# Sliding-window attention: one transposed weight tile for two key blocks, and another order for the last heads

## The chip, the cores and the metric

The kernel runs on one core of one Trainium2 chip. The metric is the device time of one execution in microseconds (us); of the kernel before, three executions are shown. The engines are named as the profile names them: PE (TensorE, matmul and transpose), PEld (its weight loads), DVE (VectorE), ACT (ScalarE), POOL (GpSimd) and SP (SyncE, which here only issues DMAs).

## The reference

The program is a decoder trunk of two layers on 1024 tokens of width 1024, all in float32. Layer 0 (RWKV-7 time mixing beside a gated MLP) isn't touched. Layer 1 is sliding-window attention with 16 query heads, 2 key/value heads, ALiBi and a learned sink per head, followed by a SiLU gate, an output projection and the final norm:

```python
q, k, v, z = jnp.split(p, [ODD_MIX, ODD_MIX + KV_W, ODD_MIX + 2 * KV_W], axis=-1)
...
dist = qi + WINDOW - kj          # qi: 0..127, kj: 0..255 (previous block, own block)
valid = (dist >= 0)[None] & (dist < WINDOW)[None] & (key_pos >= 0)
scores = scores - slopes * dist
scores = jnp.where(valid, scores, -jnp.inf)
m = jnp.maximum(jnp.max(scores, axis=-1, keepdims=True), sink)
e = jnp.exp(scores - m)
probs = e / (jnp.sum(e, axis=-1, keepdims=True) + jnp.exp(sink - m))
out = jnp.einsum('bnhgqk,bnkhd->bnqhgd', probs, v_band)
y = out * jax.nn.silu(z)
return y @ w_out
```

A block of 128 queries sees two blocks of 128 keys: the one before it and its own. Query i may use key j of the previous block only where j > i, and key j of its own block only where j <= i. So for each pair (i, j) at most one of the two weights differs from zero.

## The kernel before, in words

The change lies in layer 1, which is the last 350 us of the span. Everything is float32; a matmul operand is split into a high and a low part (`hi`/`lo`, `PH`/`PL`, `KH`/`KL`) of type float32r, and three (or two) matmuls of parts make one product.

**Tiles.** Tokens are handled in two halves of 512 (`half`), query heads in 8 pairs (`n`, two heads `e` each). `head_projs(n)` (L1361) loads the weight columns of the pair with `wload` (two DMAs of 256 KB on SP into `wraw`, of which there are three buffers; per DMA one ACT copy to `whi`, L257, and one subtraction on POOL to `wlo`, L258) and projects queries (`qproj`) and gates (`zgate`), each as 24 matmuls of 512 columns per half (`pproj`).

**One attention block** is (head pair, half, block of 128 queries), 64 in all. `attend` (L1285 on) does, for each:

1. scores: 4 matmuls `pS`;
2. bias, minimum and row maximum: 2 operations on DVE (L1305), from PSUM to `Sx`;
3. exponential with row sum: 2 on ACT (L1309);
4. reciprocal of the sums on DVE (L1311), then the scaling by it on POOL, 2 operations over all 256 keys (L1313);
5. transposes on PE, one per head and key block, 4 of 128x128 (L1319; 2 in the first block of the sequence, which has no previous block), into PSUM tile `pT`;
6. split of `pT`, 512 columns: `PH` on ACT (L1324), `PL = pT - PH` on DVE (L1325);
7. weighted sum with the values: 4 matmuls `po` of 256 columns (`PH` and `PL`, times previous and own block of `VV`; L130 is the line of the helper for all matmuls).

After two blocks, the four quadrants of `po` are put together by ACT and DVE (`cm`, L1334 to L1337) and multiplied into `y` on POOL (L1339).

**What sets the order.** A scheduler puts the instructions of each engine in one fixed order when the program is built; `attend` has high priority, so its matmuls stand between those of the projections of the next pair. At run time each engine takes its instructions in that order and waits at each for semaphores. With `N1 = 4`, half 1 of pairs 4 to 7 is attended only after all projections. The output weights (`wo`, two halves of 512 columns in `hi`/`lo` tiles that replace those of layer input `h`) are loaded after that, 8 pieces of 256 KB each (L1396 to L1398; ACT makes `hi`, POOL or DVE by turns makes `lo`). The output projection (`op`, 24 matmuls per 128 tokens and half of the columns) fills PE between the last attention blocks, and stands alone at the end.

## Time and profile before

| | |
|---|---|
| three executions | 1092.3, 1091.01, 1091.95 us; median 1091.95 us |
| the profiled execution | 1086.66 us, span 1084.8 us |
| busy in the span | PE 96%, PEld 77%, DVE 64%, ACT 48%, POOL 34% |
| transposes of attention weights on PE (L1319) | 240, mean 272 ns |
| weight scaling on POOL (L1313) | 128 |
| first score matmul, last weighted sum | at 734.8 and 1030.6 us of the span |

A row of the views that group instructions gives line, engine, operation, output tile <- input tiles and shape, the count, then the busy time in us and the mean duration in ns, then the idle time of the engine before them and what ended it. Matmuls overlap in the array: a row's mean is the duration of one, and the distance of two starts in the timeline is what one costs.

### The profile page before, as it was taken

To read this page: it belongs to the slowest core of one execution; us is meant where nothing else is said; L and a number is where in the kernel's file an instruction comes from. 1 tells how busy PE (TensorE), PEld (TensorE's weight loads), DVE (VectorE), ACT (ScalarE), POOL (GpSimd) and SP (SyncE) were. 2 spreads that over 40 slices of the span, in tenths; PEclk is the share of its full clock that TensorE was granted. 3 is DMA by queue.
4 is the path that set the end of the run, shared out by engine and by line. 5 is a ranking of instruction groups with operands and counts; after the bars stand their busy time and mean duration, and the time that the engine had idled before them with its cause. 6 is when DMAs were issued, how large, how long until landed. Compare 5 with 4: busy or idle time off the path is not lost.

```text
span 1084.8 us, 20721 instructions
## 1 busy us (share of the span) xinstructions
PE 1039.3 (96%) x7887; PEld 834.1 (77%) x7888; DVE 694.0 (64%) x1668; ACT 521.5 (48%) x1247; POOL 370.2 (34%) x483
## 2 busy tenths in 40 slices
PE   6989989998999899999999999999999999999997
PEld 3667767777777677777888787778888888878886
DVE  4355868595868585858433688755565544488753
ACT  4464464544454546454423223336665644486521
POOL 2233323232323233233344100225455544467201
PEclk9989999999999999999999999999999999999998
DMA  9601121212121122212213655411011011251221
GB/s 363 238 18 40 60 79 59 70 50 69 64 86 57 60 68 70 69 53 84 91 61 124 184 183 177 146 45 40 23 37 40 20 40 40 98 165 59 75 81 59
DMA packets 55131, 93.42 MB, mean 86 GB/s; under 512 B 5748, under 2 KB 15988, under 8 KB 55032
## 3 DMA queue, kind: packets, MB, share of 16 engines
q1 hardware_dynamic: 45176, 77.36, 21.5%
q10 hardware_dynamic: 9856, 14.75, 4.2%
q8 instruction: 62, 1.02, 0.4%
q14 instruction: 37, 0.30, 0.1%
HBM read 79.49 MB, written 12.59 MB: 85 GB/s over the span
## 4 chain that ended last, share of the span: by engine, by line
PE 52%; DVE 4%; ACT 2%; issue 1%; DMA 1%; POOL 1%; ACTq 0%; POOLq 0%; DVEq 0%; SPq 0%
PE pproj L130 24%; PE op L130 16%; PE po L130 2%; PE pS L130 2%; PE pT L1319 2%; PE htp L134 1%; PE pM L130 1%; PE py L130 0%; DVE pr L728 0%; DMA wraw<-y0d 0%; PE mix L130 0%; DVE Sx L1305 0%; PE mq L130 0%; PE gvn L130 0%; PE uw L130 0%
## 5 line engine op out<-in xcount | busy, mean ns | idle before, releaser
L130 PE MATMUL pproj<-hi,whi 128*128 128x512 f32 x696 | 281.1, 404 | 0.7 <-ACT vt L1273 0.7
L130 PE MATMUL pproj<-hi,wlo 128*128 128x512 f32 x696 | 280.7, 403 | 0.0
L130 PE MATMUL pproj<-lo,whi 128*128 128x512 f32 x696 | 280.6, 403 | 0.0
L258 POOL TENSOR_TENSOR wlo<-wraw,whi 128x512 fp32r<-128x512 f32 x86 | 114.8, 1353 | 155.2 <-ACT whi L257 154.3
L130 PEld LDWEIGHTS pproj<-hi,whi 128*128 128x128 f32 x696 | 131.4, 189 | 27.8 <-issue 3.6
L130 PEld LDWEIGHTS pproj<-hi,wlo 128*128 128x128 f32 x696 | 131.3, 189 | 26.0 <-issue 2.4
L130 PEld LDWEIGHTS pproj<-lo,whi 128*128 128x128 f32 x696 | 131.5, 189 | 25.0 <-issue 1.7
L130 PE MATMUL op<-wo,whi 128*128 128x512 f32 x256 | 81.1, 397 | 0.1
L257 ACT ACTIVATE whi<-wraw 128x512 fp32r<-128x512 f32 x102 | 59.0, 622 | 37.2 <-issue 13.5
L1309 ACT ACTIVATE Sx<-Sx,nm 128x257 f32<-128x257 f32 (+1 forms) x128 | 62.3, 489 | 27.3 <-DVE nm L1305 25.3
L1305 DVE CUSTOM_DVE_ANT_0 Sx<-pS,bias,nsink 128x256 f32<-128x256 f32 (+1 forms) x128 | 53.5, 463 | 30.0 <-PE pS L130 28.6
L1313 POOL TENSOR_SCALAR Sx<-Sx,rc 128x256 f32<-128x256 f32 (+1 forms) x128 | 60.8, 492 | 25.6 <-DVE rc L1311 23.1
L1325 DVE TENSOR_TENSOR PL<-pT,PH 128x512 fp32r<-128x512 f32 (+1 forms) x64 | 41.6, 655 | 29.7 <-ACT PH L1324 29.2
L944 DVE SCALAR_TENSOR_TENSOR adacc<-araw,cond,adacc 128x512 f32<-128x512 f32 x56 | 48.4, 864 | 19.2 <-DMA araw<-ada 19.1
L130 PEld LDWEIGHTS op<-wo,whi 128*128 128x128 f32 x256 | 47.6, 188 | 11.4 <-ACT whi L257 0.6
L130 PE MATMUL op<-hi,yh 128*128 128x512 f32 (+1 forms) x136 | 51.8, 381 | 0.4 <-ACT yh L1423 0.4
L130 PE MATMUL op<-hi,yl 128*128 128x512 f32 (+1 forms) x136 | 51.7, 380 | 0.4 <-DVE yl L1424 0.4
L130 PE MATMUL op<-lo,yh 128*128 128x512 f32 (+1 forms) x136 | 51.5, 379 | 0.0
L130 PE MATMUL op<-wo,wlo 128*128 128x512 f32 x128 | 50.8, 397 | 0.0
L1324 ACT ACTIVATE PH<-pT 128x512 fp32r<-128x512 f32 (+1 forms) x64 | 35.7, 563 | 17.4 <-PE pT L1319 16.1
L728 DVE TENSOR_TENSOR pr<-Lf,LT 128x2 f32<-128x2 f32 (+14 forms) x120 | 42.2, 352 | 2.4
L225 POOL TENSOR_TENSOR st<-st,nhalf 128x1 f32<-128x1 f32 x16 | 9.6, 601 | 96.7 <-DVE st L224 96.7
(317 smaller groups left out, 2153.2 us busy)
## 6 DMA issues: line engine op xcount, KB each, us to landing
araw<-ada SPq DMA_DIRECT2D x64, 256.0 KB, 2.7
wraw<-ew SPq DMA_DIRECT2D x50, 256.0 KB, 3.0
wraw<-ow SPq DMA_DIRECT2D x36, 256.0 KB, 2.7
adaraw<-ada SPq DMA_DIRECT2D x16, 512.0 KB, 8.4
x<-x SPq DMA_DIRECT2D x8, 512.0 KB, 9.7
woraw<-ewo SPq DMA_DIRECT2D x16, 256.0 KB, 2.9
xr<-x ACTq DMA_DIRECT2D x16, 256.0 KB, 3.8
wraw<-y0d SPq DMA_DIRECT2D x16, 256.0 KB, 3.4
```

Source lines behind the costliest of these rows:

```text
L130: last[0] = nc.tensor.matmul(out, lhsT=lhsT, rhs=rhs, **kw).ins
L134: return nc.tensor.transpose(out, in_, ident)
L257: a = S.activation(hi[:, gs, :], raws[g], AF.Copy)
L258: b = E.tensor_tensor(out=lo[:, gs, :], in0=raws[g], in1=hi[:, gs, :].bitcast(F32), op=ALU.subtract)
L728: V.tensor_tensor(out=pr[:, 0:nc_, 0:i + 1], in0=Lf[:, i:i + 1, 0:i + 1].to_broadcast([P, nc_, i + 1]), in1=LTt[:, 0:nc_, 0:i + 1], op=ALU ...
L944: op = V.scalar_tensor_tensor(out=acc, in0=raw, scalar=cond[:, k:k + 1], in1=acc, op0=ALU.mult, op1=ALU.add)
L1305: V.tensor_tensor_reduce(out=Sx[:, e, off:2 * P], in0=pS3[:, e, 0:nk], in1=bias[e][:, off:], scale=1.0, scalar=nsink[:, hd:hd + 1], op0=AL ...
L1309: S.activation(pr[:, e, off:2 * P + 1], Sx[:, e, off:2 * P + 1], AF.Exp, bias=nm[:, e:e + 1], scale=-1.0, accum_out=sm[:, e:e + 1])
L1313: G.tensor_scalar(out=pr[:, e, off:2 * P], in0=pr[:, e, off:2 * P], scalar1=rc[:, e:e + 1], scalar2=0.5, op0=ALU.mult, op1=ALU.mult)
L1319: nc.tensor.transpose(pT4[:, kb, e, :], pr[:, e, kb * P:(kb + 1) * P], ident)
L1324: S.activation(PH[:, ks, :], pT2[:, ks, :], AF.Copy)
L1325: V.tensor_tensor(out=PL[:, ks, :], in0=pT2[:, ks, :], in1=PH[:, ks, :].bitcast(F32), op=ALU.subtract)
```

## The change

Since at most one of the two weights of a pair (i, j) differs from zero, the kernel now adds the two key blocks' exponentials to one tile `F` of 128 columns per head and transposes that alone. The sum with the values becomes: `F` times the previous block's values, plus `F` times a causal 0/1 mask times the difference of own and previous values (`DV`, made once). Each of the two weight tiles is still split in two parts, so the weighted sum still has 4 matmuls of 256 columns. The work of steps 4 to 6 is put on other engines: POOL adds (one operation of 256 elements per row), ACT scales by the reciprocal (2 of 128), ACT makes `PH` and DVE `PL` of 256 columns, then POOL multiplies `PH` and DVE `PL` by the mask (256 elements each). The factor 0.5 of the old scaling goes into the values. The values' preparation gets `vf`, `dv` and `DV`, and the mask comes by a DMA on the ACT queue.

The order of the last heads changes too: `N1 = 5`; pairs 6 and 7 are projected for half 0 only; then the first half of the output weights is loaded (its tiles are free once nothing reads half 0 of `h` any more); then half 1 of pair 7, and half 1 of pair 6, whose weights are loaded a second time. The late attention blocks are those of half 1 of pairs 5, 7 and 6.

```diff
-    VV = at.tile([P, NB, 2, 2, 64], F32R, name="VV")
+    VV = at.tile([P, NB - 1, 2, 2, 64], F32R, name="VV")
+    DV = at.tile([P, NB - 1, 2, 2, 64], F32R, name="DV")
+    causal = at.tile([P, P], F32, name="causal")
+    nc.scalar.dma_start(out=causal, in_=cons[:, NC1:NC2])
...
+        vf = at.tile([P, 4, 2, 64], F32, name="vf", tag="QL", bufs=2 * (KC - 5))
+        S.activation(vf, p5, AF.Copy)
+        vfs.append(vf)
+        dv = at.tile([P, 4, 2, 64], F32, name="dv", tag="QL", bufs=2 * (KC - 5))
+        V.tensor_tensor(out=dv[:, 1:4], in0=p5[:, 1:4], in1=vf[:, 0:3], op=ALU.subtract)
+        i0 = 1 - half
+        if half:
+            V.tensor_tensor(out=dv[:, 0], in0=p5[:, 0], in1=vfs[0][:, 3], op=ALU.subtract)
+        db = slice(half * 4 - 1 + i0, half * 4 + 3)
+        S.activation(DV[:, db, :, 0, :], dv[:, i0:4], AF.Copy)
+        G.tensor_tensor(out=DV[:, db, :, 1, :], in0=dv[:, i0:4], in1=DV[:, db, :, 0, :].bitcast(F32), op=ALU.subtract)
+
+    N1 = 5
...
+                F = pr[:, :, off:off + P]
+                if b:
+                    G.tensor_tensor(out=F, in0=F, in1=pr[:, :, P:2 * P], op=ALU.add)
                 for e in range(2):
-                    G.tensor_scalar(out=pr[:, e, off:2 * P], in0=pr[:, e, off:2 * P], scalar1=rc[:, e:e + 1], scalar2=0.5, op0=ALU.mult, op1=ALU.mult)
-                nkb = nk // P
-                pT = p1("T")
-                pT4 = pT.rearrange("p (k e q) -> p k e q", k=2, e=2)
-                for kb in range(2 - nkb, 2):
-                    for e in range(2):
-                        nc.tensor.transpose(pT4[:, kb, e, :], pr[:, e, kb * P:(kb + 1) * P], ident)
+                    S.activation(F[:, e, :], F[:, e, :], AF.Copy, scale=rc[:, e:e + 1])
+                pT = p1("T")[:, 0:2 * P]
+                for e in range(2):
+                    nc.tensor.transpose(pT[:, e * P:(e + 1) * P], F[:, e, :], ident)
...
-                S.activation(PH[:, ks, :], pT2[:, ks, :], AF.Copy)
-                V.tensor_tensor(out=PL[:, ks, :], in0=pT2[:, ks, :], in1=PH[:, ks, :].bitcast(F32), op=ALU.subtract)
+                S.activation(PH[:, 0, :], pT, AF.Copy)
+                V.tensor_tensor(out=PL[:, 0, :], in0=pT, in1=PH[:, 0, :].bitcast(F32), op=ALU.subtract)
+                if b:
+                    for E, pp_ in ((G, PH), (V, PL)):
+                        E.tensor_tensor(out=pp_[:, 1, :].rearrange("p (e q) -> p e q", e=2), in0=pp_[:, 0, :].bitcast(F32).rearrange("p (e q) -> p e q", e=2),
+                                        in1=causal.unsqueeze(1).to_broadcast([P, 2, P]), op=ALU.mult)
...
+                todo = [(VV[:, b - 1 if b else 0, g, :, :], pp_[:, 0, :]) for pp_ in (PH, PL)]
+                if b:
+                    todo += [(DV[:, b - 1, g, :, :], pp_[:, 1, :]) for pp_ in (PH, PL)]
...
         wq = wload(ow[n])
-        if n < KC - 1:
-            for half in range(2):
-                qproj(n, wq, half)
+        for half in range(2 if n < KC - 2 else 1):
+            qproj(n, wq, half)
         wz = wload(ow[10 + n])
-        for half in range(2):
-            if n == KC - 1:
-                qproj(n, wq, half)
+        for half in range(2 if n < KC - 2 else 1):
             zgate(n, wz, half)
+        if n == KC - 1:
+            wo_load(0)
+            qproj(n, wq, 1)
+            zgate(n, wz, 1)
+            qproj(n - 1, wload(ow[n - 1]), 1)
+            zgate(n - 1, wload(ow[9 + n]), 1)
...
-    for n in range(N1, KC):
+    wo_load(1)
+    for n in (*range(N1, KC - 2), KC - 1, KC - 2):
         with tc.high_priority(offset=BOOST):
             attend(n, 1, qs[n, 1], biases(n))
```

`wo_load(n)` holds the old loop over the 8 pieces of one half of the output weights. The tag `Q` has 7 buffers in place of 8, and `QL` has 6 in place of 8.

Three places show what the scheduler makes of this.

On PE, in the middle of the attention (pair 1), `pT` are the transposes and `po` the weighted sums; `VV` and `DV` are the values and their differences. Before:

```order
L130 MATMUL po<-PH,VV 128x256 x2
L130 MATMUL pproj<-hi,wlo 128x512
L130 MATMUL pproj<-hi,whi 128x512
L130 MATMUL po<-PL,VV 128x256 x2
L1319 MATMUL pT<-con,Sx 128x128 x4
L130 MATMUL po<-PH,VV 128x256 x2
L130 MATMUL po<-PL,VV 128x256 x2
```

And now, at about the same place:

```order
L130 MATMUL po<-PH,VV 128x256
L130 MATMUL pS<-KH_7640,Q 128x128
L130 MATMUL pS<-KL_7642,Q 128x128
L130 MATMUL po<-PL,VV 128x256
L130 MATMUL po<-PH,DV 128x256
L130 MATMUL po<-PL,DV 128x256
L1334 MATMUL pT<-con,Sx 128x128 x2
```

A block's four transposes became two; its four weighted sums stand as before, two of them with `DV`.

On SP, at the end of its list, `ow` are columns of the input weights, `owo` pieces of the output weights. Before:

```order
L1136 DMA x1d<-xr 128x512
L247 DMA wraw<-ow 128x512
L956 DMA gated<-adacc 1x512
L247 DMA wraw<-ow 128x512 x30
L1396 DMA wraw<-owo 128x512 x16
L1452 DMA out<-xr 128x512 x8
```

And now:

```order
L1136 DMA x1d<-xr 128x512
L247 DMA wraw<-ow 128x512
L956 DMA gated<-adacc 1x512
L247 DMA wraw<-ow 128x512 x30
L1398 DMA wraw<-owo 128x512 x8
L247 DMA wraw<-ow 128x512 x4
L1398 DMA wraw<-owo 128x512 x8
L1474 DMA out<-xr 128x512 x8
```

Pair 6's weights, loaded again, stand behind the first eight pieces of the output weights and ahead of the last eight.

On PE, where the last projection has ended and the output projection `op` begins (`yh`, `yl` are the parts of `y`). Before:

```order
L130 MATMUL pS<-KH_7641,Q 128x256
L130 MATMUL pS<-KL_7643,Q 128x256
L130 MATMUL po<-PH,VV 128x256 x2
L130 MATMUL op<-hi,yh 128x512
L130 MATMUL op<-lo,yh 128x512
L130 MATMUL op<-hi,yh 128x512
L130 MATMUL op<-lo,yh 128x512
L130 MATMUL pS<-KH_7641,Q 128x256
L130 MATMUL pS<-KL_7643,Q 128x256
L130 MATMUL pS<-KH_7641,Q 128x256
L130 MATMUL pS<-KL_7643,Q 128x256
L130 MATMUL po<-PL,VV 128x256 x2
```

And now:

```order
L130 MATMUL po<-PH,VV 128x256
L1334 MATMUL pT<-con,Sx 128x128 x2
L130 MATMUL po<-PL,VV 128x256
L130 MATMUL po<-PH,DV 128x256
L130 MATMUL op<-hi,yh 128x512
L130 MATMUL op<-lo,yh 128x512
L130 MATMUL op<-hi,yl 128x512
```

Before, attention stood alone here but for four matmuls of `op`; now twenty matmuls of `op` follow each other at once, and fewer blocks are left to attend.

## The prediction, made before the result was known

> **What bounds the kernel now.** The page first, then busy time by stretch: preparation of keys and values, attention with projections beside it, the load of the output weights, attention with the output projection beside it, the end.

> ```profile
> PE 1039.3 (96%) x7887; PEld 834.1 (77%) x7888; DVE 694.0 (64%) x1668; ACT 521.5 (48%) x1247; POOL 370.2 (34%) x483
> ...
> core 0: us, PE busy (x) PEld busy (x) DVE busy (x) ACT busy (x) POOL busy (x), PEclk, DMA share, GB/s
> 700.00:735.00 35.00, 34.31 (x156) 27.18 (x155) 16.16 (x35) 11.38 (x22) 10.21 (x16) 1.00 0.21 65
> 735.00:945.00 210.00, 210.00 (x1167) 181.40 (x1166) 115.94 (x350) 121.57 (x334) 103.91 (x196) 1.00 0.12 38
> 945.00:975.00 30.00, 27.68 (x158) 23.00 (x157) 23.95 (x68) 24.83 (x66) 18.65 (x30) 1.00 0.56 180
> 975.00:1030.00 55.00, 55.00 (x314) 47.73 (x313) 45.80 (x116) 33.41 (x91) 28.58 (x52) 1.00 0.20 69
> ```

> PE is never idle from 735 to 945 and from 975 to 1030, while DVE, ACT and POOL are busy for about half of the first stretch. Only from 945 to 975 is it idle, for 30.00 - 27.68 = 2.3 us. What it waited for there:

> ```profile
> PE pS L130 <- DVE nm L1305: 0.7, 1, 0.7
> PE po L130 <- DVE PL L1325: 0.5, 1, 0.5
> PE op L130 <- DVE yl L1424: 0.4, 1, 0.4
> PE op L130 <- ACT yh L1423: 0.4, 1, 0.4
> PE po L130 <- ACT PH L1324: 0.3, 1, 0.3
> ```

> These five waits are all of PE's from 735 on. So in the layer that is changed, time is PE's list of matmuls, and an instruction taken off it is worth its distance to the next.

> **The transposes.** The granted clock is 1.00 in these stretches. Starts on PE, around the transposes of one block, and its later weighted sums:

> ```profile
> 811.05 0.60 PE L1319 MATMUL pT<-con,Sx 128*128 128x128 f32 x4
> 811.40 0.48 PE L130 MATMUL pproj<-lo,whi 128*128 128x512 f32 x1
> 811.72 0.40 PE L130 MATMUL pproj<-hi,wlo 128*128 128x512 f32 x1
> 811.96 0.40 PE L130 MATMUL pproj<-hi,whi 128*128 128x512 f32 x1
> ...
> 812.65 0.28 PE L130 MATMUL pS<-KH,Q 128*128 128x256 f32 x1
> 812.77 0.27 PE L130 MATMUL pS<-KL,Q 128*128 128x256 f32 x1
> ...
> 815.99 0.40 PE L130 MATMUL po<-PH,VV 128*128 128x256 f32 x2
> ...
> 816.81 0.48 PE L130 MATMUL po<-PL,VV 128*128 128x256 f32 x2
> ```

> Four transposes and one projection matmul take 811.72 - 811.05 = 0.67 us. A projection matmul alone takes 811.96 - 811.72 = 0.24, so four transposes take 0.43, or 0.11 each. A matmul of 256 columns takes 0.12 (812.77 - 812.65). Of 64 blocks, 56 have a previous block and lose two transposes: 112 x 0.11 = 12.3 us off PE. The weighted sums keep their count and size, so nothing comes back there.

> ```profile
> L1319 PE MATMUL pT<-con,Sx 128*128 128x128 f32 x240 | 41.1, 272 | 0.0
> ```

> This row's mean, 0.272 us, is the time from start to end of one; they overlap, and the distance decides. [...]

> **The work that goes to other engines**, per block of the 56. Means by shape:

> ```profile
> L1309 ACT ACTIVATE Sx<-Sx,nm 128x129 f32<-128x129 f32 x16 | 6.3, 395 | 3.0 <-DVE nm L1305 3.0
> L1313 POOL TENSOR_SCALAR Sx<-Sx,rc 128x256 f32<-128x256 f32 x112 | 55.1, 508 | 22.7 <-DVE rc L1311 20.4 <-DVE st L1442 1.5 <-PE pproj L130 0.6
> L1324 ACT ACTIVATE PH<-pT 128x512 fp32r<-128x512 f32 x56 | 32.7, 589 | 16.7 <-PE pT L1319 15.5 <-PE po L130 0.7
> L1324 ACT ACTIVATE PH<-pT 128x256 fp32r<-128x256 f32 x8 | 3.0, 378 | 0.7 <-PE pT L1319 0.6
> L1325 DVE TENSOR_TENSOR PL<-pT,PH 128x512 fp32r<-128x512 f32 x56 | 38.3, 688 | 28.9 <-ACT PH L1324 28.4
> L1325 DVE TENSOR_TENSOR PL<-pT,PH 128x256 fp32r<-128x256 f32 x8 | 3.4, 422 | 0.8 <-ACT PH L1324 0.7
> L1339 POOL TENSOR_TENSOR y<-y,cm 128x256 f32<-128x256 f32 x32 | 24.7, 772 | 49.7 <-DVE cm L1337 49.6
> ```

> POOL loses two scalings (2 x 0.51) and gets the add and a mask product, both of the size of L1339 (2 x 0.77): +0.52 us, 29 us over 56 blocks. ACT gets two scalings of 128 columns, at most 0.40 each (L1309's short form) and at least nothing, and saves 0.21 at `PH`: up to +0.6, 33 us in all. DVE saves 0.27 at `PL` and gets a mask product, nearest to `PL`'s short form (0.42): +0.15, 9 us. From 735 to 1030 PE covers this: POOL was busy for 104 + 19 + 29 = 152 of 295 us, ACT for 180, DVE for 186; with 29, 33 and 9 us more none comes near the 293 - 12 = 281 of PE. On PE's path it costs nothing as long as each chain ends before PE asks. The cover of the block above:

> ```profile
> 812.02 0.58 ACT L1324 ACTIVATE PH<-pT 128x512 fp32r<-128x512 f32 x1
> ...
> 812.63 0.69 DVE L1325 TENSOR_TENSOR PL<-pT,PH 128x512 fp32r<-128x512 f32 x1 [0.23 <-ACT PH L1324]
> ```

> `PH` was ready at 812.60 and used at 815.99, `PL` at 813.32 and used at 816.81: 3.4 and 3.5 us to spare. The mask adds 0.77 on POOL and 0.42 on DVE behind them. If the cover were gone, 0.77 x 56 = 43 us would be exposed.

> The values' preparation (two `vf`, two roundings of `DV` on ACT, three subtractions on DVE, two on POOL, one DMA on ACT's queue) falls in 700 to 735, where PE was busy for 34.3 of 35 us with projections and DVE, ACT and POOL for less than half; `DV` is first needed after the second block's transposes. I cost it at nothing; uncovered, one chain of it (0.59 + 0.69 + 0.59 + 1.30 by rows of 512 columns above and L258 below) is 3.2 us, once.

> **The last heads.** Pair 6's weights are loaded twice: 4 DMAs on SP, 4 ACT copies, 4 POOL subtractions, no matmul.

> ```profile
> L258 POOL TENSOR_TENSOR wlo<-wraw,whi 128x512 fp32r<-128x512 f32 x28 | 35.7, 1296 | 23.4 <-ACT whi L257 22.7 <-PE pproj L130 0.6
> ...
> L1398 POOL TENSOR_TENSOR lo<-wraw,hi x8: 1287/1294/1303, 947.9 to 982.8; 128x512 fp32r<-128x512 f32 x8
> ...
> L1398 DVE TENSOR_TENSOR lo<-wraw,hi x8: 691/874/1706, 949.3 to 981.7; 128x512 fp32r<-128x512 f32 x8
> ```

> On SP the reload stands behind eight pieces of the output weights, and all pass through three `wraw` buffers. Sixteen pieces took from 947.9 to 982.8 + 1.3 before, or 2.26 us each. The split of the output weights can begin when pair 7's gate, half 0, is projected; query half 1 of pair 6 then needs ten pieces: 22.6 us. In the changed order PE has until then 48 matmuls of 512 columns, 56 of 256, 4 of 128 and 12 transposes: 48 x 0.23 + 56 x 0.12 + 4 x 0.06 + 12 x 0.11 = 19.3 us. That is 3.3 us late. Likewise, from the last projection to the last piece of the second output half PE has 45 matmuls of 512, 37 of 256 and 10 transposes, 15.9 us, against 8 x 2.26 = 18.1: 2.2 late. These 5.5 us are an upper figure; the lower is nothing, since before's pace was itself held up by dense attention. Three pieces fit into the buffers ahead of time in each case, so I take 7/10 of the one and 5/8 of the other: 2.3 + 1.4 = 3.7. On the other side, the 2.3 us of 945 to 975 can go: that stretch was attention almost without other matmuls, and now projections or `op` stand between. I take all of it.

> **Sum.** 12.3 + 2.3 - 3.7 = 10.9 us less, between 12.3 - 5.5 = 6.8 and 12.3 + 2.3 = 14.6. The profiled execution took 1086.66 us (span 1084.8 and 1.9 around it), so it becomes 1075.8. The median of the three runs is 1091.95, 5.3 above that execution; less 10.9 it is 1081.0 (1081.05).

> **Rivals.**

> *DVE and POOL block one another: slower.* The mask product is a DVE operation with both inputs in SBUF, which steps 2 to 7 of a block did not have. Such operations and POOL's did hold each other up:

> ```profile
> 947.87 2.56 POOL L1398 TENSOR_TENSOR lo<-wraw,hi 128x512 fp32r<-128x512 f32 x2 [3.36 <-ACT hi L1397]
> ...
> 949.27 1.71 DVE L1398 TENSOR_TENSOR lo<-wraw,hi 128x512 fp32r<-128x512 f32 x1
> ...
> 945.00:975.00 30.00, 4.48 (x20) 3.33 (x20) 0.84 (x2) 1.52 (x4) 1.00 0.56 180
> ```

> The DVE subtraction that takes 0.69 alone took 1.71, until POOL's pair had ended at 950.43 and half a microsecond on. [...] Now 56 mask products on DVE meet 112 new operations on POOL. From 945 to 975, where eight such DVE subtractions began to meet POOL, 20 weighted sums (five blocks) cost PE 2.3 us of idle time, 0.46 per block. If all 56 blocks paid that, 25.8 us would come on: 1091.95 - 12.3 + 25.8 = 1105. It decides against the change from (12.3 + 2.2) / 56 = 0.26 us per block. Against it speak the 3.4 us of cover and the shorter hold (256 elements, not 512). I give it 0.08.

> *The reload is later than summed.* If the three buffers pass a piece per 2.39 to 2.64 us, not 2.26, the eighteen pieces take 43.0 to 47.6 us, 7.8 to 12.4 more than PE's 19.3 + 15.9: of 14.6 us a gain of 6.8 to 2.2 is left, 1085.2 to 1089.7. For it: POOL's subtractions now stand among adds and mask products. Chance 0.14. Stalls that just eat the gain, 12.4 to 16.8 us, are no change: 0.05.

> *A transpose is worth its 0.27 us*, or other waits go too: 112 x 0.272 = 30.5, 1061.5. The distances above speak against it; 0.05 for a gain over 14.6.

> **How the numbers follow.** Forecast 0.68, with its own range 1077.4 to 1085.2; with the small gains and the large ones, faster is 0.68 + 0.14 + 0.05 = 0.87. A difference under 0.2%, 2.2 us, can't be told from none: same 0.05, slower 0.08. The range 1076 to 1087.5 leaves out slower, same, the smallest gains (0.05) and the largest (0.02): 0.20.

> **What would show it.** Right: 128 transposes at L1334 at the same distance, PE still idle for under 6 us from 735 to the end of attention, `po` with `DV` seldom waiting. The reload shows as waits of PE or PEld for `wlo` or `whi` of pair 6. Wrong: `po` waiting for mask products at L1341 through the whole stage, mask products on DVE well over 0.42 us, or PE's idle time over 12 us.

## The result, and the profile after

| | kernel before | changed kernel |
|---|---|---|
| executions shown with the change | 1091.95 us median (1090.88 to 1094.52, 5 runs) | 1082.88 us median (1080.95 to 1087.42, 5 runs) |
| ratio of the times, 95% interval | | 0.9918 [0.989, 0.9946] |
| the profiled execution | 1086.66 us, span 1084.8 | 1081.32 us, span 1078.8 |
| first score matmul to last matmul of the layer | 735.01 to 1076.91: 341.90 us | 738.21 to 1071.52: 333.31 us |

The change is worth 9.1 us here. In a second measurement the same kernel gave 0.9953 [0.9931, 0.9974], 4.3 us (below). Executions of one kernel lie up to 12 us apart (1078.24 to 1090.58 in the second measurement), and part of that falls ahead of the attention: in the profiles of this case the first score matmul starts between 733.3 and 739.9. So the last row, called the stage from here on, is taken from each profile beside the median: 8.6 us less here, 4.1 less in the profile of the second measurement.

From the page of the changed kernel its first line, then three of the prediction's stretches, in the columns shown there:

```profile
PE 1031.4 (96%) x7776; PEld 824.6 (76%) x7776; DVE 714.6 (66%) x1727; ACT 551.8 (51%) x1383; POOL 405.5 (38%) x471
```

```profile
735.00:945.00 210.00, 210.00 (x1153) 180.41 (x1152) 141.52 (x435) 156.34 (x473) 136.12 (x200) 1.00 0.15 47
945.00:975.00 30.00, 26.98 (x147) 22.38 (x145) 25.31 (x77) 29.24 (x88) 26.40 (x39) 0.96 0.30 98
975.00:1030.00 55.00, 55.00 (x264) 46.21 (x264) 41.98 (x88) 26.42 (x70) 23.66 (x28) 0.96 0.29 97
```

From 735 to 945 PE is still never idle, though DVE, ACT and POOL work 26, 35 and 32 us more than before: the cover holds. From 945 to 975 PE is idle for 3.0 us, where 2.3 were to go, and the granted clock, 1.00 before, is 0.96. All waits of PE in the stage:

```profile
PE op L130 <- DVE y L1363: 1.2, 1, 1.2
PE pT L1334 <- DVE rc L1326: 1.1, 1, 1.1
PE pS L130 <- DVE Q L1374: 0.4, 2, 0.2
PE pS L130 <- DVE nm L1320: 0.4, 1, 0.4
```

No row names a reloaded weight, a piece of the output weights or a mask product. The operations of a block, by groups (POOL's sum and mask, ACT's scaling, DVE's mask and split, PE's transposes):

```profile
L1329 POOL TENSOR_TENSOR Sx<-Sx 128x256 f32<-128x256 f32 x56 | 42.2, 755 | 11.4 <-ACT Sx L1324 10.7
L1341 POOL TENSOR_TENSOR PH<-PH,causal 128x256 fp32r<-128x256 f32 x56 | 46.1, 825 | 18.9 <-ACT PH L1337 18.5
L1331 ACT ACTIVATE Sx<-Sx,rc 128x128 f32<-128x128 f32 x128 | 43.7, 393 | 5.8 <-POOL Sx L1329 4.6 <-DVE rc L1326 0.7
L1341 DVE TENSOR_TENSOR PL<-PL,causal 128x256 fp32r<-128x256 f32 x56 | 35.0, 629 | 1.1
L1338 DVE TENSOR_TENSOR PL<-pT,PH 128x256 fp32r<-128x256 f32 x64 | 26.8, 421 | 11.4 <-ACT PH L1337 8.3 <-ACT Sx L1331 1.4 <-PE po L130 0.4
L1334 PE MATMUL pT<-con,Sx 128*128 128x128 f32 x128 | 26.6, 272 | 1.1 <-DVE rc L1326 1.1
```

DVE's mask (629 ns) and split (421 ns) do the same amount of work; what lengthens the one is below. The place where PE waits, in the timelines of PE and of DVE of the changed kernel (start, duration, then the operation; idle time before it in brackets):

```profile
972.20 0.42 PE L1334 MATMUL pT<-con,Sx 128*128 128x128 f32 x2 [1.09 <-DVE rc L1326]
...
974.20 0.80 PE L130 MATMUL op<-hi,yh 128*128 128x512 f32 x1 [1.16 <-DVE y L1363]
...
978.64 0.63 PE L130 MATMUL op<-lo,yh 128*128 128x512 f32 x1
979.07 0.50 PE L130 MATMUL op<-hi,yl 128*128 128x512 f32 x1
...
979.86 0.40 PE L130 MATMUL op<-hi,yl 128*128 128x512 f32 x1
980.10 0.39 PE L130 MATMUL op<-hi,yh 128*128 128x512 f32 x1
```

```profile
970.49 1.23 DVE L1446 TENSOR_TENSOR yl<-y,yh 128x1024 fp32r<-128x1024 f32 x1 [0.21 <-issue]
...
971.97 0.15 DVE L1326 RECIPROCAL rc<-sm 128x2 f32<-128x2 f32 x1
972.49 1.07 DVE L1439 TENSOR_TENSOR gate<-gate,gateb 128x512 f32<-128x512 f32 x1 [0.36 <-DMA gateb<-rows]
973.48 0.67 DVE L1363 SCALAR_TENSOR_TENSOR y<-zth,pproj 128x512 f32<-128x512 f32 x1
```

Two things follow one another. The transposes wait while DVE makes `yl` for the output projection and, behind it, `PL` and `rc`. Then DVE itself waits for the DMA of `gateb`, a part of the output gate that is added to `gate`; `y` stands behind that sum, and `op` starts as soon as `y` has been made (in the code, `op` shares two PSUM tiles with the projections, and `y` reads one of them). The matmuls of `op` then start 0.43 us apart until 979 and 0.23 from 979.4 on. The stretch by itself:

```profile
965.00:972.50 7.50, 6.22 (x35) 5.02 (x34) 6.02 (x15) 7.44 (x20) 5.02 (x9) 1.00 0.27 75
972.50:979.30 6.80, 5.64 (x15) 4.29 (x15) 4.92 (x8) 4.46 (x12) 5.87 (x6) 0.50 0.49 152
```

The granted clock is halved (0.50) for 6.83 us, from 972.47 on. That is after the wait of the transposes and before the wait for `y`, which starts at 973.05; so in this execution the first of the two waits came ahead of it, and the second fell into it. The eleven steps of `op` from 974.20 to 979.07 took 4.87 us; at 0.23 each they take 2.5. So the halved clock cost 2.3 us on top of the waits. In the 3.41 us before 972.47 PE was idle for 1.28 us; what made the clock fall there isn't shown.

### The profile page after: what moved, and what is told of

The parts are those of the page before. It is cut to its first block, busy times and chain, and to the rows that moved or that the text cites. A ratio compares the mean times of both kernels' runs of the same rounds, so it can differ in the third digit from the quotient of the medians.

```text
span 1078.8 us, 20631 instructions
## 1 busy us (share of the span) xinstructions
PE 1031.4 (96%) x7776; PEld 824.6 (76%) x7776; DVE 714.6 (66%) x1727; ACT 551.8 (51%) x1383; POOL 405.5 (38%) x471
## 4 chain that ended last, share of the span: by engine, by line
PE 49%; DVE 4%; DMA 3%; ACT 2%; issue 1%; POOL 0%; POOLq 0%; ACTq 0%; DVEq 0%; SPq 0%
PE pproj L130 25%; PE op L130 14%; PE pS L130 2%; PE po L130 2%; PE pT L1334 1%; DMA araw<-ada 1%; DMA wraw<-owo 1%; PE htp L134 1%; PE pM L130 1%; DVE pr L728 1%; PE py L130 0%; DMA wraw<-y0d 0%; DVE adacc L944 0%; PE mix L130 0%; PE mq L130 0%
## 5 line engine op out<-in xcount | busy, mean ns | idle before, releaser
L130 PE MATMUL pproj<-hi,whi 128*128 128x512 f32 x696 | 282.5, 406 | 0.7 <-ACT vt L1277 0.7
L130 PE MATMUL pproj<-lo,whi 128*128 128x512 f32 x696 | 281.4, 404 | 0.0
L130 PE MATMUL pproj<-hi,wlo 128*128 128x512 f32 x696 | 281.3, 404 | 0.0
L258 POOL TENSOR_TENSOR wlo<-wraw,whi 128x512 fp32r<-128x512 f32 x90 | 121.2, 1364 | 145.5 <-ACT whi L257 145.4
L130 PEld LDWEIGHTS pproj<-hi,whi 128*128 128x128 f32 x696 | 131.8, 189 | 28.2 <-issue 4.0
L130 PEld LDWEIGHTS pproj<-hi,wlo 128*128 128x128 f32 x696 | 131.7, 189 | 26.4 <-issue 2.4
L130 PEld LDWEIGHTS pproj<-lo,whi 128*128 128x128 f32 x696 | 132.1, 190 | 25.2 <-issue 1.7
L130 PE MATMUL op<-wo,whi 128*128 128x512 f32 x256 | 81.1, 397 | 0.1
L257 ACT ACTIVATE whi<-wraw 128x512 fp32r<-128x512 f32 x106 | 61.3, 622 | 25.6 <-PE pproj L130 12.4
L1324 ACT ACTIVATE Sx<-Sx,nm 128x257 f32<-128x257 f32 (+1 forms) x128 | 62.1, 488 | 12.7 <-DVE nm L1320 12.3
L130 PEld LDWEIGHTS op<-wo,whi 128*128 128x128 f32 x256 | 47.6, 188 | 11.3 <-ACT whi L257 0.5
L130 PE MATMUL op<-hi,yh 128*128 128x512 f32 (+1 forms) x136 | 52.4, 385 | 1.2 <-DVE y L1363 1.2
L1341 POOL TENSOR_TENSOR PH<-PH,causal 128x256 fp32r<-128x256 f32 x56 | 46.1, 825 | 18.9 <-ACT PH L1337 18.5
L130 PE MATMUL op<-hi,yl 128*128 128x512 f32 (+1 forms) x136 | 52.4, 385 | 0.0
L130 PE MATMUL op<-lo,yh 128*128 128x512 f32 (+1 forms) x136 | 52.3, 384 | 0.0
L130 PE MATMUL op<-wo,wlo 128*128 128x512 f32 x128 | 50.8, 397 | 0.0
L1331 ACT ACTIVATE Sx<-Sx,rc 128x128 f32<-128x128 f32 x128 | 43.7, 393 | 5.8 <-POOL Sx L1329 4.6
L1329 POOL TENSOR_TENSOR Sx<-Sx 128x256 f32<-128x256 f32 x56 | 42.2, 755 | 11.4 <-ACT Sx L1324 10.7
```

The lines of the kernel that those rows point to most:

```text
L130: last[0] = nc.tensor.matmul(out, lhsT=lhsT, rhs=rhs, **kw).ins
L257: a = S.activation(hi[:, gs, :], raws[g], AF.Copy)
L258: b = E.tensor_tensor(out=lo[:, gs, :], in0=raws[g], in1=hi[:, gs, :].bitcast(F32), op=ALU.subtract)
L1324: S.activation(pr[:, e, off:2 * P + 1], Sx[:, e, off:2 * P + 1], AF.Exp, bias=nm[:, e:e + 1], scale=-1.0, accum_out=sm[:, e:e + 1])
L1329: G.tensor_tensor(out=F, in0=F, in1=pr[:, :, P:2 * P], op=ALU.add)
L1331: S.activation(F[:, e, :], F[:, e, :], AF.Copy, scale=rc[:, e:e + 1])
```

## The experiments

The theory: the transposes taken off give their 12 us, the order its part, and what is missing is lost near the last projection, to DVE's waits and the halved clock. Rivals: the reload; DVE and POOL holding each other up, called the lock below (before, the subtractions of L1398 took DVE 0.69 us at the least and 1.71 beside two of POOL); a transpose's price of 0.27 us. The runs were made in three groups, each timed against the kernel before on one chip: its medians were 1089.08 us (30 runs) for the sum alone to no reload, 1088.93 (18) for the changed kernel again, the first gate sum on POOL and the masks, and 1089.48 (17) for the rest; the changed kernel as first shown has its own, 1091.95. Stage and idle time (of PE, from the first score matmul on) are from one profile each; half clock is its length within the stage.

| kernel | median us (runs) | ratio, 95% interval | stage us | PE idle us | half clock us |
|---|---|---|---|---|---|
| before, third group | 1089.48 (17) | 1 | 341.90 (the profile shown) | 2.32 | 0 |
| changed, as first shown | 1082.88 (5) | 0.9918 [0.989, 0.9946] | 333.31 | 3.03 | 6.83 |
| changed, again | 1084.65 (12) | 0.9953 [0.9931, 0.9974] | 337.78 | 6.04 | 10.24 |
| sum alone | 1084.26 (7) | 0.995 [0.993, 0.9971] | 336.35 | 5.87 | 6.83 |
| order alone | 1086.13 (12) | 0.997 [0.9951, 0.999] | 338.63 | 0.24 | 0 |
| four transposes | 1089.28 (12) | 0.9998 [0.998, 1.0017] | 342.39 | 2.08 | 0 |
| no reload | 1085.85 (12) | 0.9964 [0.9944, 0.9984] | 337.77 | 6.39 | 6.83 |
| gate sum on POOL | 1077.66 (6) | 0.9903 [0.9876, 0.9929] | 334.12 | 4.10 | 3.41 |
| the same, again | 1078.8 (6) | 0.9904 [0.9878, 0.993] | 333.55 | 3.33 | 3.41 |
| masks on DVE | 1080.83 (7) | 0.9931 [0.9905, 0.9956] | 333.89 | 5.86 | 0 |
| masks on POOL | 1079.73 (6) | 0.9923 [0.99, 0.9945] | 333.34 | 4.96 | 0 |
| before, gate sum on POOL | 1086.75 (12) | 0.9979 [0.9959, 0.9999] | 340.93 | 1.95 | 0 |
| gate sum and output weights on POOL | 1078.55 (6) | 0.9904 [0.9873, 0.9934] | 332.86 | 3.92 | 0 |
| gate sum and masks on POOL | 1075.31 (5) | 0.9875 [0.9847, 0.9904] | 328.55 | 1.33 | 0 |

**The sum alone.** The changed kernel (its `N1 = 5` too) with the order of before:

```diff
-        if n == KC - 1:
-            wo_load(0)
...
-    for n in (*range(N1, KC - 2), KC - 1, KC - 2):
+    for n in range(N1, KC):
```

> The summed weight tile alone; the projections of the last pairs and the load of the output weights as before (half 1 of pair 4 is attended early, as in the change). Theory (the gain is 112 transposes off PE at 0.11 us each, whatever the order of the last heads): 8 to 12 us less than before, 0.989 to 0.993. Rival (the order of the last heads makes the gain, the saving of the transposes is eaten by the new work on POOL and DVE): within 3 us of before, 0.997 to 1.003.

0.995 lies between the two. PE's largest wait in its stage, and what DVE did ahead of it:

```profile
PE pS L130 <- DVE nm L1320: 3.2, 2, 2.4
...
```

```profile
966.90 1.05 DVE L1434 TENSOR_TENSOR gate<-gate,gateb 128x512 f32<-128x512 f32 x1 [1.12 <-DMA gateb<-rows]
967.88 0.68 DVE L1363 SCALAR_TENSOR_TENSOR y<-zth,pproj 128x512 f32<-128x512 f32 x1
```

Here too DVE waits for the DMA of `gateb`, and the gate's sum, the last `y` and behind it the operations on the scores come late; for these PE waits 2.4 us, until 969.41. So with the order of before the gate's sum stands in front of `y` as well.

Idle time grew by 5.87 - 2.32 = 3.6 us, and the clock was halved for 6.83 us from 969.03, within that wait. With 12.3 us for the transposes and 2.3 for the clock, as in the changed kernel, that makes -12.3 + 3.6 + 2.3 = -6.4; the stage is 5.6 us shorter. The gain of the transposes is there, and half of it is lost between 964 and 981 us.

**The order alone.** The kernel before with the new order, the reload and `N1 = 5`, and four transposes as before.

> The other order of the last heads alone; four transposes per block and the work of the engines as before. Theory: PE's list is as long as before, and at most the 2.3 us of idle time from 945 to 975 can go: 0.998 to 1.002. Rival (the order makes the gain): 7 to 10 us less, 0.991 to 0.994.

0.997, between the two: 3.3 us of stage, more than the theory's 2.3. PE has one wait left in the stage:

```profile
PE op L130 <- POOL lo L1383: 0.2, 1, 0.2
```

On DVE the gate's sum stands behind the last `y` here, as before:

```profile
979.39 0.68 DVE L1346 SCALAR_TENSOR_TENSOR y<-zth,pproj 128x512 f32<-128x512 f32 x1
...
980.79 0.82 DVE L1422 TENSOR_TENSOR gate<-gate,gateb 128x512 f32<-128x512 f32 x1
```

So in this order the 2.3 us of waits do go, and the reload, with the split of the output weights beside it, costs 0.2 us of waiting. The two parts, 5.6 and 3.3 us of stage, make 8.9, against 8.6 for both in the first profile and 4.1 in the second; that they add up is not shown.

**Four transposes.** The changed kernel, with two more transposes of `F` per block into a part of `pT` that nothing reads:

```diff
+                if b:
+                    for e in range(2):
+                        nc.tensor.transpose(pT[:, (2 + e) * P:(3 + e) * P], F[:, e, :], ident)
```

> The changed kernel with two more transposes in each of the 56 blocks, into columns that nothing reads; all other work stays. Theory: 112 x 0.11 = 12.3 us come back, 1.000 to 1.004 of before. If transposes were priced by their duration of 0.27 us: 30 us come back, 1.019. If they are hidden beside other work: 0.992 as the changed kernel.

```profile
L1337 PE MATMUL pT<-con,Sx 128*128 128x128 f32 x112 | 21.8, 272 | 0.0
```

With the transposes back, and all the rest of the change in place, the time is that of before (0.9998). So without the transposes' gain nothing is left of the change, and nothing of the 3.3 us of the order alone either. At 0.27 us each, 112 of them would have made the stage 30 us longer than the changed kernel's. It is 9.1 longer; with 2.3 for the half clock that it doesn't have and 0.95 for its shorter idle time that is near 12.3.

**No reload.** Half 1 of pair 6 takes pair 7's weights, so its queries and gates are computed with other weights; two loads go.

```diff
-            qproj(n - 1, wload(ow[n - 1]), 1)
-            zgate(n - 1, wload(ow[9 + n]), 1)
+            qproj(n - 1, wq, 1)
+            zgate(n - 1, wz, 1)
```

> The changed kernel without the second load of pair 6's weights: half 1 of pair 6 is projected with pair 7's weights, so its values differ. Theory (no wait of PE in the trace names the reloaded weights, so they cost nothing): as the changed kernel, 0.990 to 0.993. Rival (the prediction's term: the reload is 2 to 4 us late): 2 to 4 us less than the changed kernel, 0.987 to 0.990.

Neither: it is no faster. Its largest wait:

```profile
PE po L130 <- DVE PL L1341: 3.3, 2, 2.8
...
```

The scheduler laid the end out in another way, and DVE is late elsewhere: PE waits for a mask product that takes DVE 0.43 us but starts late, at 1000.15, behind `yl` and other work. The gate's sum stands behind the last `y` here (975.49 and 974.89). As a measure of the reload it is inconclusive; that the reload isn't waited for is shown by the waits of the changed kernel and of the order alone.

**The changed kernel again**, beside the next three.

> The changed kernel once more, beside the three variants of it on one chip. Both theories: 0.989 to 0.995 of the time before; from the first score matmul to the last matmul of the layer 333 to 336 us. If the half-speed stretch of the granted clock near 972 us of the span belongs to this order of instructions, it is there again behind a gap of PE of over 1 us; if it fell there by chance, the stage takes about 2.4 us less without it.

0.9953 and 337.8 us, just outside. DVE, then PE, at the same place as above:

```profile
973.23 1.25 DVE L1446 TENSOR_TENSOR yl<-y,yh 128x1024 fp32r<-128x1024 f32 x1 [0.27 <-issue]
...
975.89 1.65 DVE L1439 TENSOR_TENSOR gate<-gate,gateb 128x512 f32<-128x512 f32 x1 [1.00 <-DMA gateb<-rows]
977.47 0.67 DVE L1363 SCALAR_TENSOR_TENSOR y<-zth,pproj 128x512 f32<-128x512 f32 x1
```

```profile
978.19 0.80 PE L130 MATMUL op<-hi,yh 128*128 128x512 f32 x1 [2.58 <-DVE y L1363]
```

Instruction by instruction the same, but the DMA lands 0.7 us later behind the start of `yl` and the sum takes 1.65 us, not 1.07. `op` waits 2.6 us, and within that wait, at 976.31, the clock is halved again for 6.83 us (3.41 more are at 955.83). So one kernel's stage differs by 4.5 us between two executions, by waits and clock at its end.

**The gate's sum on POOL**, twice:

```diff
-        V.tensor_tensor(out=gate[n], in0=gate[n], in1=gb[n], op=ALU.add)
+        G.tensor_tensor(out=gate[n], in0=gate[n], in1=gb[n], op=ALU.add)
```

> The sum of the gate's two parts moves from DVE to POOL (8 operations in this layer, 64 in neither path of the transposes). Theory: near the last projection PE waits for DVE, which has the gate's sum in front of the y that the output projection needs; with the sum on POOL the wait of 1.2 us for y goes, and with it the clock's half-speed stretch: 2 to 4 us less than the changed kernel, 0.986 to 0.992 of the time before. Rival: POOL, itself busy there with the subtractions of the output weights, makes the sum as late as DVE did: within 1 us of the changed kernel.

> The changed kernel with the gate's sum on POOL, once more. Theory (DVE's wait for the gate's DMA held y up): 0.988 to 0.993 of the time before, as in its first measurement, and no wait of PE for y at L1363 longer than 0.5 us. Rival (its first measurement was a lucky one, since its stage time was only 3.7 us under that of the changed kernel beside it, its median 7.0): 0.993 to 0.996.

0.9903 and 0.9904, as the theory said both times (the sum is 2 operations, not the 8 that the expectation names). The waits of the first:

```profile
PE po L130 <- DVE PL L1338: 1.2, 1, 1.2
PE pT L1334 <- DVE rc L1326: 1.1, 1, 1.1
PE pS L130 <- DVE nm L1320: 0.8, 2, 0.4
PE po L130 <- ACT PH L1337: 0.5, 1, 0.5
PE pT L1334 <- ACT Sx L1331: 0.2, 1, 0.2
PE op L130 <- DVE lo L1400: 0.2, 1, 0.2
```

The wait for `y` is gone, and so is the half clock at that place, though the wait of 1.1 us ahead of the transposes is still there; the other, 3.41 us at 957.9, stays. Against the changed kernel of the same group (0.9953, 337.78 us) the intervals don't overlap. Against its first measurement (0.9918 [0.989, 0.9946], 333.31 us) they do, and the two stages here, 334.12 and 333.55 us, are no shorter. So the move takes the wait for `y` away; how much that gives on average isn't shown.

**The kernel before with the gate's sum on POOL**, the same edit of one line:

> The kernel before with the gate's sum on POOL. Theory (the sum stands ahead of what PE needs only in the changed order): within 0.2% of the kernel before, 0.998 to 1.002. Rival (the sum on DVE costs in any order): 0.993 to 0.997.

0.9979 [0.9959, 0.9999] lies 0.0001 outside the theory's range and nearer to it than to the rival's; the stage is 1.0 us shorter. Before, DVE made that sum without waiting, after the last `y`:

```profile
967.44 0.68 DVE L1346 SCALAR_TENSOR_TENSOR y<-zth,pproj 128x512 f32<-128x512 f32 x1
...
969.94 0.68 DVE L1417 TENSOR_TENSOR gate<-gate,gateb 128x512 f32<-128x512 f32 x1
```

So there the sum costs little, 0.2% at this median. What counts is its place in DVE's list. It stands ahead of the last `y` in the changed kernel and in the sum alone, and behind it before, in the order alone, with four transposes and without the reload. (With both masks on one engine it stands ahead too, but there PE had `op` to do already and didn't wait for that `y`.) So the new order of the heads by itself didn't put it there; why the scheduler did isn't shown.

**Both masks on DVE, both on POOL.** `for E, pp_ in ((G, PH), (V, PL))` becomes `((V, PH), (V, PL))`, or `((G, PH), (G, PL))`.

> Both mask products of a block on DVE, none on POOL. DVE gets 56 x 0.42 = 24 us more, POOL loses 56 x 0.82 = 46 us. Theory (the lock of DVE and POOL is there, but the 3.5 us ahead of the weighted sums cover it): PE's busy time from 745 to 945 us stays at 200, the time within 2 us of the changed kernel (0.990 to 0.994 of before), the mask products on DVE nearer to 0.42 us than with POOL's beside them (0.606 median). Rival (DVE is near its limit and bounds the blocks): PE waits for L1341 on DVE in many blocks, 5 us or more over the changed kernel.

> Both mask products of a block on POOL, none on DVE, so that a block has no operation left on DVE with both inputs in SBUF. Theory of the lock: POOL's mask products fall from 0.825 us towards the 0.755 us of its add or below, since nothing on DVE holds them up; POOL's load is 56 x 0.75 = 42 us more, about 440 of 1080 us, and the second product ends 0.75 us later than the first: covered, the time within 2 us of the changed kernel. Rival (POOL bounds the blocks): the weighted sums with the low part wait for POOL at L1341 through the stage, 56 x 0.2 us or more, 10 us over the changed kernel.

Both stay near the changed kernel or better, with PE at 200.00 of the 200 us from 745 to 945. By groups, first of the kernel with both on DVE, then with both on POOL:

```profile
L1341 DVE TENSOR_TENSOR PL<-PL,causal 128x256 fp32r<-128x256 f32 x56 | 32.6, 583 | 0.3
L1341 DVE TENSOR_TENSOR PH<-PH,causal 128x256 fp32r<-128x256 f32 x56 | 30.8, 551 | 1.7 <-ACT PH L1337 1.6
```

```profile
L1341 POOL TENSOR_TENSOR PH<-PH,causal 128x256 fp32r<-128x256 f32 x56 | 42.2, 755 | 8.6 <-ACT PH L1337 7.8
L1341 POOL TENSOR_TENSOR PL<-PL,causal 128x256 fp32r<-128x256 f32 x56 | 41.3, 740 | 3.4 <-DVE PL L1338 3.2
```

With no such operation on DVE, POOL's mask takes 0.755 us, not 0.825. With both on DVE, 44 of the 112 masks ran in a time without any POOL operation and took 0.415 us on average, and the other 68 took 0.665. In the changed kernel all 56 masks of DVE ran beside an operation of POOL (629 ns on average). So the two engines do hold each other up, by 0.07 us of POOL's and some 0.2 of DVE's mask, and neither way of dividing the masks makes the blocks wait from 745 to 945. Their medians are 4 to 5 us under that of the changed kernel on the same chip, but the intervals overlap with its interval.

**Two more pieces off DVE**, on top of the gate's sum: the four subtractions of the first half of the output weights that DVE made (`V if k % 2 and n else G`), or both masks.

> Changed kernel with the gate's sum and all eight subtractions of the first half of the output weights on POOL (four were on DVE, one of which took 1.8 us near 951 us of the span and had the PL that the weighted sum waited for behind it). Theory (DVE's subtraction is what PE waited for there): the wait of 1.2 us for PL at L1338 goes, 330 to 333 us of stage, 0.986 to 0.991 of before. Rival (POOL, at 1.29 us for each subtraction, now delays the sums of the two key blocks): waits for POOL at L1329 or L1400 take its place, 334 us or more.

> Changed kernel with the gate's sum and both mask products of a block on POOL. Theory (the stalls around the last projection come from DVE): PE idle for under 3 us from the first score matmul on, no half-speed stretch of the clock there, 328 to 332 us from the first score matmul to the last matmul, 0.985 to 0.990 of before. Rival (with DVE freed POOL holds the chain up there): waits of PE for POOL at L1341 or L1329, 333 us or more, 0.990 to 0.995.

The first removes the wait for `PL`, as expected, and gets waits of 0.8 to 1.2 us for `lo`, `hi` and `op` in its place: 0.9904 and 332.86 us are at the theory's upper ends, and no gain over the gate's sum alone. The second is the fastest kernel here, 0.9875, with a stage of 328.55 us as the theory had it. Its first two stretches and all its waits:

```profile
735.00:945.00 210.00, 210.00 (x1157) 180.41 (x1156) 118.63 (x398) 156.98 (x480) 162.30 (x246) 1.00 0.15 52
945.00:975.00 30.00, 29.34 (x166) 24.91 (x164) 23.97 (x71) 29.00 (x87) 28.20 (x41) 1.00 0.25 82
```

```profile
PE pproj L130 <- DVE Q L1374: 0.5, 1, 0.5
PE op L130 <- POOL lo L1400: 0.4, 1, 0.4
PE op L130 <- ACT hi L1399: 0.2, 1, 0.2
PE op L130 <- ACT op L1460: 0.2, 1, 0.2
```

POOL is busy for 162 of 210 us, DVE for 119, PE waits 1.3 us, and the clock stays at 1.00 through the stage. The scheduler also set the end in another order (`op` starts at 966.0, among the last projections), so not all of its lead over the other kernels is DVE's relief alone.

## Why the prediction was right, and where it wasn't

The forecast was 10.9 us less; the two measurements are 9.1 and 4.3. The first lies between the ends of the sum, 6.8 and 14.6, the second below them: the mechanism was right, and the losses beside it were under-sized.

- **The transposes, -12.3 us: right, shown.** The stage without its idle time can be compared where the clock isn't halved. In four kernels with two transposes (masks on DVE, masks on POOL, and the gate sum on POOL with the output weights or with the masks) it is 327.2 to 328.9 us; in the four with four transposes (before, with the gate sum on POOL, the order alone, four transposes) it is 338.4 to 340.3. The means are 11.2 us apart, 0.10 us for each of 112; any one of the first four and any one of the others are 9 to 13 apart. Two transposes more undo the gain. The weighted sums gave nothing back.
- **The work on other engines at nothing: right from 735 to 945, wrong behind.** The prices were near (POOL 0.755 and 0.825 us against 0.77, ACT 0.393 against at most 0.40, DVE's split 0.421 against 0.42); DVE's mask took 0.629 against 0.42, which the prediction had named as a sign of being wrong. It cost nothing in the dense part, where PE waits for none of this work. From 945 on DVE was the latest in most waits of PE, in the changed kernel and in the sum alone.
- **The idle time of 945 to 975, -2.3 us: the step that failed.** "I take all of it" holds for the order alone (0.24 us left). Together with the sum, idle time rose, by 0.7 us in one execution and 3.7 in the other. The prediction added up DVE's work and did not ask what stands ahead of what PE needs next in DVE's list: the gate's sum, with its DMA, came ahead of the last `y`. PE waited 1.2 and 2.6 us behind it in the two executions of the changed kernel, and 2.4 us in the sum alone; with the sum on POOL that wait is gone. The other wait of the first profile, 1.1 us for the transposes, comes from `yl` on DVE and stays with the sum on POOL.
- **The reload, +3.7 us: not found.** No wait of PE in the changed kernel names it, nor the second half of the output weights; in the order alone all idle time is 0.24 us. The lower end, nothing, fits better. The kernel without the reload could not settle it.
- **Not in the sum: the clock**, +2.3 us in the profile shown, more in the second one (10.24 us of half clock). -12.3 + 0.7 + 2.3 = -9.3, where the stage has -8.6; the last 0.7 us is within what the transposes' 12.3 is uncertain by.

So a loss of 3.7 us that didn't come stood in for another that did, of 0.7 + 2.3 + 2.3 = 5.3 against the forecast's terms; the agreement in the first measurement is partly luck.

Of the rivals, DVE and POOL do hold each other up, and that costs the blocks nothing in the dense part; the time of 1105 would have needed PE to wait in every block, and it waits in none from 735 to 945. A mask took POOL 0.825 us in the changed kernel and 0.755 with none on DVE; with both on DVE it took DVE 0.665 us beside an operation of POOL and 0.415 without. At the end, beside POOL, the gate's sum took 1.07 and 1.65 us where it took 0.68 before, so POOL may have a share in the wait for `y`. "Reload later" falls with the missing waits, the price of 0.27 us with the four transposes.

## What to carry to other kernels

An instruction taken off an engine that never waits is worth its distance to the next one (here 0.10 us for each of 112 transposes, whose mean duration is 0.272), and the work pushed to others is free only while each chain has time to spare (here from 735 to 945, where PE was busy for 210.00 of 210 us, and no longer from 945 on): look for the place where the dense part ends, and read there, engine by engine, what stands ahead of the results that the busy engine needs next. DVE took its list in order here: in the changed kernel's second profile the gate's sum waited 1.00 us for its DMA and took 1.65, `y` came behind it, and PE waited 2.58 us for that. So an operation that waits for a DMA should not stand in front of those results. Beside the waits themselves, look at the clock: in six of the profiles here it fell to half after 1.28 to 2.81 us of idle time of PE in 3.41 us, which in the changed kernel cost 2.3 us more; in the kernel before, with 2.32 us in the whole stage, it didn't fall.

## What was not expected of the hardware

```profile
994.53 0.36 PE L130 MATMUL po<-PH,VV 128*128 128x256 f32 x1 [2.81 <-ACT op L1460]
994.73 0.39 PE L130 MATMUL op<-hi,yh 128*128 128x512 f32 x1
994.95 0.39 PE L130 MATMUL op<-lo,yh 128*128 128x512 f32 x1
```

  There `op` goes on at 0.22 us. So the length of a wait alone doesn't decide it; what else does stays open.
- The first gate sum on DVE took 0.68 us before, and 1.07 and 1.65 us in two executions of the changed kernel. In these two POOL had an operation with inputs in SBUF under way as the sum began: an addition that ended 0.5 us later, and a subtraction that ended 1.1 us later. That POOL's operation is what held DVE up is the likely reading; no run changes that alone for this sum.
